# Turning two heads' marks and maxima at a time in an attention stage, with a new order of its look-ahead

## The chip, the cores and the metric

The kernel runs on one core of a Trainium2 chip. The metric is the device time of one execution in microseconds (us); lower is better. The engines are named as in the profile: PE is the tensor engine (PEld its weight loads), ACT the scalar engine, DVE the vector engine, POOL the GpSimd engine, SP the one that issues DMAs here.

## The reference

One decoder layer on x (1, 1024, 1024) in float32. After a modulated layer norm one projection gives all inputs of two attention sides and their gates:

```python
u = _layer_norm(x) * (1.0 + scale[:, None, :]) + shift[:, None, :]
(q_a, kv_cmp, kv_sel, kv_win, g_nsa, z_a,
 q_b, kv_b, z_b, g_merge) = _split_columns(u @ w_in[l])
...
o_cmp, p_cmp = _compressed_attention(qa, kc, vc)
sel_idx = _select_blocks(p_cmp, S)
o_sel = _selected_attention(qa, k_s, v_s, sel_idx)
o_win = _banded_attention(qa, k_w, v_w, NSA_WINDOW)
...
o_b = _banded_attention(qb, k_b, v_b, SWA_WINDOW, sinks[l]).reshape(B, S, SWA_WIDTH)
y_b = o_b * jax.nn.silu(z_b)
merged = jax.nn.sigmoid(gm_a) * (y_a @ w_up_a[l]) + jax.nn.sigmoid(gm_b) * (y_b @ w_up_b[l])
out = merged @ w_out[l]
x = _layer_norm(DEEPNORM_ALPHA * x + gate[:, None, :] * out) * ln_g[l] + ln_b[l]
```

Side a has 8 query heads in 2 groups of 4 (64 columns each) and three branches: compressed keys, the 8 best blocks of 64 keys, and a window of 512 keys. Side b has 8 heads in 2 groups, a window of 128 keys, and a sink for each head. All scores are scaled by 0.125 before their softmax.

## The kernel before

**Stages.** The layer norm and the first projections run until about 140 us. Then comes attention, until about 725 us, then the gating of its outputs, the two up projections, the output projection and the last norm.

**Units.** Attention works through 32 units in a fixed order: side a, group 0, query tiles 0 to 7 (128 rows each), then group 1, then the same for side b. A unit holds 4 heads. It has three parts.

- `C` turns the queries. ACT rounds them into `qat` and POOL puts what rounding leaves beside it; four transposes on PE (L759) give `qa`, copied by ACT (L761). In side a it then does the compressed branch: scores, a softmax over 64 columns, and for query tiles 4 and up the choice of blocks, whose marks (0 or -1e30 for 16 blocks) POOL writes into `qbt`.
- `M` finds each row's maximum: matmuls of `qa` with the keys, then DVE's passes over them (L878) and a reduction (L882) that writes the negated maxima of two branches into two columns of `qbt`. Then four transposes (L890), one for each head, and a copy by ACT (L892) give `qb`. Each of the two tiles `qbt` is 128 x (4 heads x 128): 64 columns of rounded queries (written by ACT, L755), 16 of marks, 2 of maxima, the rest zeros.
- For each tile of 128 keys, `score` makes two matmuls over all four heads, one of the keys' high parts with `qa` and one with `qb`, whose further rows add marks and maxima. Masked tiles get a pass of DVE (L907) and the exp by ACT (L909); others the exp alone (L911). ACT rounds the result to `ph` (L914) and POOL takes the rest `pl` (L917). `weigh` multiplies both with the values, and `combine` writes the unit's result.

**Order.** `run` emits these parts. While unit i is weighed, step by step, `part` emits a share of `M` for unit i + 1 and of `C` for unit i + 2, and both are finished with the unit. Each step also reports a planned time (0.43 for a score, 0.54 for a weighing, 0.22 for 512 columns of maxima, 0.25 for turning), and `feed` multiplies it with a ratio and emits that much of *fill*: matmuls that attention does not wait for (the next group's query projections, side b's keys and values, and blocks of 128 columns of the gates' projection). A fill block loads its weights with DMAs through three buffers, ACT rounds them (L259), POOL takes the rest (L260). `ratio` is 9.0 before the first unit, 0.9 in it, 1.25 in the rest of side a; in side b it spreads what is left over the remaining need. Four of the gates' blocks are kept for the stage after attention. A planner in the compiler then orders the instructions on each engine, with this order of emission as their priority.

Before the first unit, `values` brings the values of two branches to a common scale and splits them (four passes of ACT, four of DVE). The queries' rotation tables are scaled by 0.125 when they are made (L1173).

Of the kernel before, what the change touches and what calls it, by code (L numbers as in the profile page):

```python
# [20 lines left out]
NT = 8  # L21
# [6 lines left out]
POFF = math.log(16.0)  # L28
XB = 8
# [25 lines left out]
RATIO = {'start': 9.0, 'e': 0.9, 'a': 1.25, 'b': 1.0}  # L55
EU = 1
# [659 lines left out]
class Att:  # L716


    def __init__(self, L, q, work):

        self.L, self.q, self.w = L, q, work
        self.ms, self.st, self.av = Banks(L, MS), Banks(L, ST), Banks(L, (5,))
        nc = L.nc
        self.nc = nc
        self.U = {}
        self.qbt = []
        for i in range(2):
# [3 lines left out]
        self.p0 = work.tile([128, 128], F32, name="p0")[:, :68]  # L731
        nc.gpsimd.memset(self.p0, 0.0)
        self.n, self.last = 0, []
        self.off = [True, True]

    def rows_off(self, i):

        if not self.off[i]:
            self.nc.gpsimd.tensor_copy(self.qbt[i][:, :, 64:80],
                                       self.L.mk[:, 128:129, None].to_broadcast([128, 4, 16]))  # L740
            self.off[i] = True


    def C(self, u):
# [6 lines left out]
        qbt = st["qbt"] = self.qbt[self.n % 2]  # L751
# [3 lines left out]
        (nc.gpsimd.tensor_copy if QL == 2 else nc.scalar.copy)(qbt[:, :, 0:64], q)  # L755
# [4 lines left out]
        qa = st["qa"] = w.tile([128, 512], F32R, name="qa", tag="qa", bufs=3)  # L760
        nc.scalar.copy(qa, tr.bitcast(F32).rearrange("p h t -> p (h t)"))  # L761
        yield 0.25
        if side == "b":
            self.rows_off(self.n % 2)
            return
# [11 lines left out]
        nc.scalar.activation(e, t, AF.Exp)  # L777
# [4 lines left out]
        pc = w.tile([128, 4, 64], F32, name="cp", tag="cp")  # L782
# [25 lines left out]
        pT = w.tile([128, 2, 128], F32, name="pT", tag="pT")  # L808
# [20 lines left out]
    def M(self, u):  # L829
# [3 lines left out]
        qa, qbt = st["qa"], st["qbt"]  # L833
# [48 lines left out]
        nc.vector.tensor_reduce(qbt[:, :, 80:82], mx, axis=AX.X, op=OP.max, negate=True)  # L882
        if side == "b":
            es = st["es"] = w.tile([128, 2, 4], F32, name="esink", tag="esink", bufs=3)
            nc.gpsimd.tensor_tensor(es[:, 0], L.sink[:, g * 4:g * 4 + 4], qbt.bitcast(F32)[:, :, 80 + g], op=OP.add)
            nc.scalar.activation(es[:, 1], es[:, 0], AF.Exp, bias=L.poff)
        yield 0
        tr = self.ms.tile([128, 4, 128], F32R)
        for h in range(4):
            self.last.append(nc.tensor.transpose(tr[:, h, :], qbt[:, h, :], L.idr).ins)  # L890
        qb = st["qb"] = w.tile([128, 512], F32R, name="qb", tag="qb", bufs=2)
        nc.scalar.copy(qb, tr.bitcast(F32).rearrange("p h t -> p (h t)"))  # L892
        yield 0.25


    def score(self, u, br, kt):
# [9 lines left out]
        if kt == qt or edge:  # L906
            nc.vector.tensor_tensor(e.rearrange("p (h q) -> p h q", h=4), ps.rearrange("p (h q) -> p h q", h=4),  # L907
                                    L.mkt[:, int(edge), None, :].to_broadcast([128, 4, 128]), op=OP.add)
            nc.scalar.activation(e, e, AF.Exp, bias=L.poff)  # L909
        else:  # L910
            nc.scalar.activation(e, ps, AF.Exp, bias=L.poff)  # L911
# [48 lines left out]
    def run(self, units, fill, ratio, values):  # L960
# [52 lines left out]

        def part(f, u, k, n):
# [26 lines left out]
        for gi, grp in enumerate(groups):  # L1041
            u, bi = steps[grp[0]][:2]
            ui = units.index(u)
            side = "e" if ui < EU else u[0]
# [21 lines left out]
            if k == n:  # L1066
                if ui + 1 < len(units):
                    finish(self.M, units[ui + 1])
                if ui + 2 < len(units):
                    finish(self.C, units[ui + 2])  # L1070
# [53 lines left out]
def run_layer(L):  # L1124
# [22 lines left out]
    nc.sync.dma_start(L.sink, bass.AP(tensor=I["sinks"].tensor, offset=I["sinks"].offset, ap=[[0, 128], [1, 8]]))  # L1147
    acc = L.acc1
# [45 lines left out]
    def q_chunk(side, g, rows):  # L1194
# [3 lines left out]
        for t in ORD[side][g]:  # L1198
# [5 lines left out]
            L.rope(q, a[:, :256], t, qp, nc.vector, L.qcos, L.qsin)  # L1204
# [96 lines left out]
    for cm in (wk_cm, kvb[0], k0_cm, k1_cm, qp_cm):  # L1301
        L.close(cm)
# [214 lines left out]
```

## Time and profile before

| | us |
|---|---|
| median of 3 runs | 943.93 |
| lowest, highest | 943.79, 946.45 |
| the profiled execution | 945.29 |
| its span, first to last instruction | 943.5 |
| PE busy in the span | 914.3 |
| POOL, DVE, ACT busy | 575.6, 550.2, 471.4 |

The profiled execution is one run of its own; its time and its span differ by what lies before the first and after the last instruction. A busy time is the union of an engine's instructions. The ends of PE's matmuls are modelled, so a busy PE may still start its matmuls a little late. In the rows below, idle time stands ahead of the instruction that ended it, with the engine and line that released it.

### The profile page before, as it was taken

To read this page: it belongs to the slowest core of one execution; us is meant where nothing else is said; L and a number is where in the kernel's file an instruction comes from. 1 tells how busy PE (TensorE), PEld (TensorE's weight loads), DVE (VectorE), ACT (ScalarE), POOL (GpSimd) and SP (SyncE) were. 2 spreads that over 40 slices of the span, in tenths; PEclk is the share of its full clock that TensorE was granted. 3 is DMA by queue.
4 is the path that set the end of the run, shared out by engine and by line. 5 is a ranking of instruction groups with operands and counts; after the bars stand their busy time and mean duration, and the time that the engine had idled before them with its cause. 6 is when DMAs were issued, how large, how long until landed. Compare 5 with 4: busy or idle time off the path is not lost.

```text
span 943.5 us, 18610 instructions
## 1 busy us (share of the span) xinstructions
PE 914.3 (97%) x6592; PEld 787.0 (83%) x6592; DVE 550.2 (58%) x1621; ACT 471.4 (50%) x984; POOL 575.6 (61%) x808
## 2 busy tenths in 40 slices
PE   7899998999999999999999999999899999999996
PEld 5689997788899888898899888789788888888885
DVE  7843356554776554465786643456552666454687
ACT  5846344344555566646555555756663664532100
POOL 7867565365768766767677766756753245535822
PEclk9999999999999999999999999999989999999999
DMA  9913232212202211202201212030222977655312
GB/s 329 293 29 115 81 91 57 79 51 79 68 7 53 62 57 57 63 13 70 76 7 35 74 58 75 22 101 13 69 62 75 371 249 221 192 188 193 130 69 110
DMA packets 93278, 95.40 MB, mean 101 GB/s; under 512 B 7616, under 2 KB 72192, under 8 KB 93184
## 3 DMA queue, kind: packets, MB, share of 16 engines
q1 hardware_dynamic: 93184, 94.21, 31.9%
q8 instruction: 52, 0.85, 0.4%
q14 instruction: 42, 0.34, 0.1%
HBM read 73.21 MB, written 20.97 MB: 100 GB/s over the span
## 4 chain that ended last, share of the span: by engine, by line
PE 69%; DMA 8%; DVE 8%; POOL 7%; ACT 3%; issue 3%; SPq 1%; DVEq 0%; POOLq 0%; ACTq 0%
PE bank L108 65%; DMA sg<-gm_raw 2%; POOL z L1421 2%; DMA raw<-in_w_ada_dram 2%; DMA raw<-in_w_out_dram 1%; DMA raw<-in_w_in_dram 1%; POOL rstd L1444 1%; DVE res L1450 1%; POOL pl L917 1%; PE bank L890 1%; DVE jk L878 1%; DMA x<-in_x_dram 1%; PE bank L759 1%; POOL whl L260 1%; PE bank L1327 1%
## 5 line engine op out<-in xcount | busy, mean ns | idle before, releaser
L108 PE MATMUL bank<-whl,uH 128*128 128x256 f32 (+3 forms) x1168 | 270.6, 322 | 4.6 <-ACT uH L449 4.3
L108 PE MATMUL bank<-uH,whl 128*128 128x512 f32 x768 | 247.5, 397 | 0.0
L917 POOL TENSOR_TENSOR pl<-e,ph 128x512 f16<-128x512 f32 x162 | 188.1, 1167 | 66.4 <-ACT ph L914 58.1
L108 PEld LDWEIGHTS bank<-whl,uH 128*128 128x128 f32 x1168 | 197.9, 189 | 22.2 <-ACT uH L449 5.3
L108 PE MATMUL bank<-whl,uL 128*128 128x256 f32 (+3 forms) x584 | 181.3, 319 | 0.0
L108 PEld LDWEIGHTS bank<-uH,whl 128*128 128x128 f32 x768 | 142.1, 189 | 26.8
L260 POOL TENSOR_TENSOR whl<-raw,whl 128x256 fp32r<-128x256 f32 x128 | 99.1, 779 | 86.6 <-ACT whl L259 78.6
L108 PE MATMUL bank<-uL,whl 128*128 128x512 f32 x384 | 151.3, 394 | 0.0
L108 PEld LDWEIGHTS bank<-whl,uL 128*128 128x128 f32 x584 | 110.1, 189 | 7.4
L914 ACT CAST ph<-e 128x512 f16<-128x512 f32 x162 | 98.4, 618 | 25.1 <-PE bank L108 23.1
L878 DVE CUSTOM_DVE_ANT_0 jk<-bank,mk 128x256 bf16<-128x256 f32 (+3 forms) x168 | 73.9, 440 | 30.0 <-PE bank L108 25.4
L911 ACT ACTIVATE e<-bank,poff 128x512 f32<-128x512 f32 x92 | 62.0, 687 | 54.0 <-PE bank L108 50.3
L108 PEld LDWEIGHTS bank<-uL,whl 128*128 128x128 f32 x384 | 72.6, 189 | 14.9
L259 ACT CAST whl<-raw 128x256 fp32r<-128x256 f32 x128 | 50.8, 404 | 66.0 <-PE bank L108 42.2
L108 PE MATMUL bank<-yH,whl 128*128 128x512 f32 x256 | 79.1, 393 | 0.0
L108 PEld LDWEIGHTS <-pl 128*128 128x128 f16 x648 | 59.4, 98 | 17.1 <-issue 11.2
L249 POOL TENSOR_TENSOR whl<-raw,whl 128x256 fp32r<-128x256 f32 (+3 forms) x60 | 53.3, 895 | 24.1 <-ACT whl L248 22.8
L907 DVE TENSOR_TENSOR e<-bank,mkt 128x512 f32<-128x512 f32 x70 | 47.5, 688 | 33.0 <-PE bank L108 27.9
L108 PEld LDWEIGHTS <-ph 128*128 128x128 f16 x1296 | 65.2, 97 | 0.8 <-issue 0.5
L909 ACT ACTIVATE e<-e,poff 128x512 f32<-128x512 f32 x70 | 49.8, 721 | 30.5 <-DVE e L907 30.2
L248 ACT CAST whl<-raw 128x256 fp32r<-128x256 f32 (+3 forms) x72 | 34.2, 480 | 60.9 <-DMA raw<-in_w_out_dram 36.8
L108 PEld LDWEIGHTS bank<-yH,whl 128*128 128x128 f32 x256 | 47.7, 188 | 10.1 <-issue 0.5
(292 smaller groups left out, 1730.0 us busy)
## 6 DMA issues: line engine op xcount, KB each, us to landing
raw<-in_w_in_dram SPq DMA_DIRECT2D x136, 128.0 KB, 2.2
gm_raw<-gmo SPq DMA_DIRECT2D x48, 256.0 KB, 2.0
wada<-in_w_ada_dram SPq DMA_DIRECT2D x16, 512.0 KB, 6.0
sg<-gm_raw SPq DMA_DIRECT2D x32, 256.0 KB, 3.2
x<-in_x_dram SPq DMA_DIRECT2D x8, 512.0 KB, 5.1
o_raw<-q SPq DMA_DIRECT2D x32, 128.0 KB, 1.9
o<-o_raw SPq DMA_DIRECT2D x8, 512.0 KB, 6.7
z<-gm_raw SPq DMA_DIRECT2D x16, 256.0 KB, 6.7
```

The source lines that it names most:

```text
L108: return self.nc.tensor.matmul(out, l, r, start=start, stop=stop, skip_group_check=True)
L248: self.cast = nc.scalar.copy(h, raw).ins
L249: low = eng.tensor_tensor(l, raw, h.bitcast(F32), op=OP.subtract).ins
L259: nc.scalar.copy(hl[:, 0], raw)
L260: eng.tensor_tensor(hl[:, 1], raw, hl.bitcast(F32)[:, 0], op=OP.subtract)
L878: nc.vector.tensor_tensor_reduce(o, src, m, 1.0, -3e38, OP.add, OP.max, mx[:, h, g if side == "b" else bi, slots[h]:slots[h] + 1])
L907: nc.vector.tensor_tensor(e.rearrange("p (h q) -> p h q", h=4), ps.rearrange("p (h q) -> p h q", h=4), L.mkt[:, int(edge), None, :].to_bro ...
L909: nc.scalar.activation(e, e, AF.Exp, bias=L.poff)
L911: nc.scalar.activation(e, ps, AF.Exp, bias=L.poff)
L914: nc.scalar.copy(ph, e)
L917: eng.tensor_tensor(pl, e, ph, op=OP.subtract)
L1421: nc.gpsimd.tensor_scalar(z[:, t, :], z[:, t, :], ALPHA, None, op0=OP.mult)
```

## The change

Marks and maxima get a small tile of their own. `ex` is 128 x (4 heads x 32): 16 columns of marks, 2 of maxima, the rest zeros. Two heads are turned by one transpose, which gives 64 rows, and two copies by ACT put them into rows 64 to 95 of `qb`. The rounded queries no longer go through a second transpose: `C` copies them from its own transposes into rows 0 to 63 of `qb`, beside the copy that makes `qa`. `qb` is now one of three standing tiles (four in side b), whose rows 64 to 127 are cleared once, by DVE.

The scale of 0.125 moves from the rotation tables into the exps, and the sinks are divided by it once.

The scratch tiles of side a's compressed branch go to a pool of their own, which is closed when side b's first queries are turned; a fourth `qb`, a third `ex` and a fourth `qa` take its place.

The order: the first unit's `M` is emitted ahead of `values`. From side b's first unit on, while unit i is weighed, `M` of i + 1 is finished (its transposes and copies), `M` of i + 2 is emitted without them (`all_but`), and `C` of i + 3 is emitted. The fill's ratio is 1.5 in the first unit, 1.8 in side a's other units with query tile 0 to 3, and 1.05 in the rest of side a. The planned time for turning marks and maxima is 0.14.

```diff
-RATIO = {'start': 9.0, 'e': 0.9, 'a': 1.25, 'b': 1.0}
+RATIO = {'start': 9.0, 'e': 1.5, 's': 1.8, 'a': 1.05, 'b': 1.0}
...
-        self.qbt = []
-        for i in range(2):
-            q = work.tile([128, 4, 128], F32R, name=f"qbt{i}")
-            nc.gpsimd.tensor_copy(q.rearrange("p h d -> p (h d)"), L.mk[:, 128:129].to_broadcast([128, 512]))
-            self.qbt.append(q)
+
+        self.ex = [work.tile([128, 4, 32], F32R, name=f"ex{i}") for i in range(2)]
+        self.qb = [work.tile([128, 512], F32R, name=f"qb{i}") for i in range(3)]
+        for x in self.ex:
+            nc.gpsimd.tensor_copy(x.rearrange("p h c -> p (h c)"), L.mk[:, 128:129].to_broadcast([128, 128]))
+        for x in self.qb:
+            nc.vector.tensor_copy(x[64:128], L.mk[64:128, 128:129].to_broadcast([64, 512]))
...
-        qbt = st["qbt"] = self.qbt[self.n % 2]
+        if side == "a":
+            ex, qb = self.ex[self.n % 2], self.qb[self.n % 3]
+        else:
+            if len(self.ex) == 2:
+
+                L.close(self.wx_cm)
+                self.wx, self.wx_cm = L.pool("sideb", 1, side="right")
+                self.qb.append(self.wx.tile([128, 512], F32R, name="qb3"))
+                self.ex.append(self.wx.tile([128, 4, 32], F32R, name="ex2"))
...
-        (nc.gpsimd.tensor_copy if QL == 2 else nc.scalar.copy)(qbt[:, :, 0:64], q)
         yield 0
...
         nc.scalar.copy(qa, tr.bitcast(F32).rearrange("p h t -> p (h t)"))
+        nc.scalar.copy(qb[0:64], tr.bitcast(F32)[0:64].rearrange("p h t -> p (h t)"))
         yield 0.25
...
-        tr = self.ms.tile([128, 4, 128], F32R)
-        for h in range(4):
-            self.last.append(nc.tensor.transpose(tr[:, h, :], qbt[:, h, :], L.idr).ins)
-        qb = st["qb"] = w.tile([128, 512], F32R, name="qb", tag="qb", bufs=2)
-        nc.scalar.copy(qb, tr.bitcast(F32).rearrange("p h t -> p (h t)"))
-        yield 0.25
+        tr = self.ms.tile([128, 2, 128], F32R)
+        for j in range(2):
+            self.last.append(nc.tensor.transpose(tr[0:64, j, :], ex[:, 2 * j:2 * j + 2, :].rearrange("p h c -> p (h c)"),
+                                                 L.idr).ins)
+        rows = qb[64:96].rearrange("p (j i t) -> p i j t", j=2, i=2)
+        for i in range(2):
+            nc.scalar.copy(rows[:, i], tr.bitcast(F32)[i * 32:i * 32 + 32])
+        yield 0.14
...
-            nc.scalar.activation(e, ps, AF.Exp, bias=L.poff)
+            nc.scalar.activation(e, ps, AF.Exp, bias=L.poff, scale=SCALE)
...
+        def all_but(f, u):
+
+            s = get(f, u)
+            while s[1] < 3:
+                s[1] += 1
+                feed(next(s[0]))
...
+        def jobs(ui):
+
+            b = 2 * NT
+            if ui == b - 2:
+                return [(finish, self.C, b + 1, 0)]
+            if ui == b - 1:
+                return [(finish, self.M, b, -6), (finish, self.C, b + 2, -3), (all_but, self.M, b + 1, -1)]
+            if ui >= b:
+                e = EORD
+                return [(finish, self.M, ui + 1, e[0]), (all_but, self.M, ui + 2, e[1]), (finish, self.C, ui + 3, e[2])]
+            return []
+
         side = "start"
         finish(self.C, units[0])
+        finish(self.M, units[0])
         values()
         finish(self.C, units[1])
-        finish(self.M, units[0])
...
-            side = "e" if ui < EU else u[0]
+            side = "e" if ui < EU else "s" if u[0] == "a" and u[2] < 4 else u[0]
...
-            if ui + 1 < len(units):
+            if ui < 2 * NT - 1:
                 part(self.M, units[ui + 1], k, n)
-            if ui + 2 < len(units):
                 part(self.C, units[ui + 2], k, n)
+            for f, g, x, w in jobs(ui):
+                if x < len(units) and k == (w if w > 0 else n + w):
+                    f(g, units[x])
...
+    nc.gpsimd.tensor_scalar(L.sink, L.sink, 1.0 / SCALE, None, op0=OP.mult)
...
-    L.qcos = qp.tile([128, 8, 32], F32, name="qcos")
-    qsin = qp.tile([128, 2, 8, 32], F32, name="qsin")
-    L.qsin = (qsin[:, 0], qsin[:, 1])
-    for o, x in ((L.qcos, L.cos), (L.qsin[0], L.nsin), (L.qsin[1], L.sin)):
-        nc.scalar.mul(o, x, 0.125)
...
-            L.rope(q, a[:, :256], t, qp, nc.vector, L.qcos, L.qsin)
+            L.rope(q, a[:, :256], t, qp, nc.vector)
```

## Rows read from the trace of the kernel before

**Rows 1.** The page's first part: busy time of each engine in us, share of the span, instructions.

```profile
PE 914.3 (97%) x6592; PEld 787.0 (83%) x6592; DVE 550.2 (58%) x1621; ACT 471.4 (50%) x984; POOL 575.6 (61%) x808
```

**Rows 2.** Busy time of each engine (PE, PEld, DVE, ACT, POOL, with instructions) in stretches of attention and after it; then granted clock, DMA share, GB/s. The second number is the stretch's length.

```profile
140.00:200.00 60.00, 55.25 (x334) 46.92 (x333) 35.41 (x117) 25.48 (x56) 30.30 (x48) 1.00 0.23 60
200.00:600.00 400.00, 399.37 (x3472) 346.54 (x3471) 234.29 (x841) 224.54 (x443) 274.87 (x358) 1.00 0.18 53
600.00:675.00 75.00, 72.81 (x714) 64.99 (x713) 43.19 (x163) 49.42 (x106) 51.47 (x81) 1.00 0.16 47
675.00:700.00 25.00, 22.40 (x154) 18.22 (x153) 12.70 (x42) 15.27 (x33) 14.97 (x25) 0.86 0.26 70
700.00:725.00 25.00, 24.59 (x189) 20.41 (x189) 9.19 (x35) 11.02 (x23) 11.06 (x15) 1.00 0.19 53
725.00:900.00 175.00, 175.00 (x802) 144.71 (x801) 100.46 (x146) 70.82 (x133) 84.69 (x68) 1.00 0.65 214
```

**Rows 3.** The same view in three steps of 5 us inside side b; the number after POOL's is the granted clock.

```profile
680.00:685.00 5.00, 2.48 (x13) 1.96 (x14) 1.70 (x9) 4.63 (x11) 3.42 (x7) 0.83 0.34 81
685.00:690.00 5.00, 5.00 (x24) 4.04 (x24) 2.94 (x8) 3.47 (x7) 4.03 (x7) 0.50 0.00 0
690.00:695.00 5.00, 5.00 (x57) 4.07 (x55) 1.75 (x8) 1.60 (x4) 1.48 (x2) 0.98 0.32 105
```

**Rows 4.** Side b, 603 to 722 us: the stretch as a whole, then PE's groups there with count, busy us, mean ns, idle us before them and who ended that.

```profile
603.00:722.00 119.00, 114.12 (x993) 99.23 (x994) 64.02 (x235) 72.88 (x154) 74.69 (x117) 0.97 0.19 54
...
L108 PE MATMUL bank<-Vw,pl 128*128 128x65 f16 x72 | 8.8, 198 | 0.5 <-POOL pl L917 0.5
...
L108 PE MATMUL bank<-Vs,pl 128*128 128x65 f16 x60 | 7.0, 195 | 0.5 <-POOL pl L917 0.5
L890 PE MATMUL bank<-idr,qbt 128*128 128x128 f32 x56 | 6.8, 244 | 1.4 <-DVE qbt L882 1.4
L108 PE MATMUL bank<-Kw,qa 128*128 128x256 f32 (+1 forms) x32 | 6.6, 295 | 1.5 <-ACT qa L761 1.5
L759 PE MATMUL bank<-idr,qat 128*128 128x128 f32 x52 | 6.6, 246 | 1.2 <-DVE mx L878 1.2
```

**Rows 5.** Instructions in order of time at the start of attention (start us, us, engine, line, operation; in brackets the idle time before and who ended it).

```profile
140.98 1.16 POOL L729 CAST qbt<-mk 128x512 fp32r<-128x512 f32 x2
...
143.07 0.37 PE L759 MATMUL bank<-idr,qat 128*128 128x128 f32 x2 [0.79 <-POOL qat L753]
...
158.17 1.34 ACT L334 ACTIVATE Vs<-vrs,vmxs 128x512 f16<-128x512 f32 x2
...
161.55 0.71 PE L108 MATMUL bank<-vcb,pT 128*128 128x128 f32 x4 [1.52 <-ACT pT L809]
...
189.94 0.54 PE L890 MATMUL bank<-idr,qbt 128*128 128x128 f32 x4 [0.63 <-DVE qbt L882]
```

**Rows 6.** The same view of PE, around transposes of L890: a pair and four, each with the matmul that starts next.

```profile
601.12 0.29 PE L890 MATMUL bank<-idr,qbt 128*128 128x128 f32 x2
601.24 0.34 PE L759 MATMUL bank<-idr,qat 128*128 128x128 f32 x2
...
672.36 0.46 PE L890 MATMUL bank<-idr,qbt 128*128 128x128 f32 x4
672.66 0.21 PE L108 MATMUL bank<-Vw,pl 128*128 128x65 f16 x1
```

**Rows 7.** Groups of the whole span by line, tiles and shape: count, busy us, mean ns, idle before.

```profile
L892 ACT CAST qb<-bank 128x512 fp32r<-128x512 f32 x32 | 18.8, 586 | 22.4 <-PE bank L890 22.2
...
L890 PE MATMUL bank<-idr,qbt 128*128 128x128 f32 x128 | 15.8, 245 | 2.0 <-DVE qbt L882 2.0
...
L755 ACT CAST qbt<-q 128x256 fp32r<-128x256 f32 x32 | 13.1, 409 | 0.1
...
L809 ACT COPY pT<-bank 128x256 f32<-128x256 f32 x16 | 5.9, 369 | 14.1 <-PE bank L807 14.1
...
L309 ACT CAST Kw<-bank 64x256 fp32r<-64x256 f32 x12 | 4.4, 364 | 5.5 <-DVE Kw L308 5.3
```

**Rows 8.** ACT in order of time in side b, and the PE row that follows.

```profile
680.37 0.40 ACT L259 CAST whl<-raw 128x256 fp32r<-128x256 f32 x1 [1.48 <-DMA raw<-in_w_in_dram]
680.68 0.72 ACT L909 ACTIVATE e<-e,poff 128x512 f32<-128x512 f32 x1
681.30 0.56 ACT L761 CAST qa<-bank 128x512 fp32r<-128x512 f32 x1
...
681.92 0.50 PE L108 MATMUL bank<-Kw,qa 128*128 128x256 f32 x2 [1.55 <-ACT qa L761]
```

**Rows 9.** The first scaling of the rotation tables (duration ns min/median/max, start us), and POOL's sum of sinks and maxima in side b.

```profile
L1173 ACT ACTIVATE qcos<-cos x1: 413/413/413, 63.4 to 63.4; 128x256 f32<-128x256 f32 x1
...
L885 POOL TENSOR_TENSOR esink<-sink,qbt 128x4 f32<-128x4 f32 x14 | 2.9, 204 | 2.7 <-DVE qbt L882 2.7
```

**Rows 10.** ACT's groups in side b, 603 to 722 us, with the idle time before them.

```profile
L909 ACT ACTIVATE e<-e,poff 128x512 f32<-128x512 f32 x31 | 21.7, 720 | 16.3 <-DVE e L907 16.2
...
L892 ACT CAST qb<-bank 128x512 fp32r<-128x512 f32 x15 | 8.8, 585 | 8.4 <-PE bank L890 8.2
L761 ACT CAST qa<-bank 128x512 fp32r<-128x512 f32 x14 | 8.1, 578 | 5.3 <-PE bank L759 5.3
L259 ACT CAST whl<-raw 128x256 fp32r<-128x256 f32 x17 | 6.8, 405 | 11.2 <-PE bank L108 6.0 <-DMA raw<-in_w_in_dram 5.0
```

More of the change, by code (lines that the diff above doesn't have):

```diff
@@ L28 @@
 POFF = math.log(16.0)
+SCALE = 0.125
+EORD = (1,0,1)
 XB = 8
@@ L725, in __init__ @@
         self.U = {}
-        self.qbt = []
-        for i in range(2):
-            q = work.tile([128, 4, 128], F32R, name=f"qbt{i}")
-            nc.gpsimd.tensor_copy(q.rearrange("p h d -> p (h d)"), L.mk[:, 128:129].to_broadcast([128, 512]))
-            self.qbt.append(q)
+        self.ex = [work.tile([128, 4, 32], F32R, name=f"ex{i}") for i in range(2)]
[4 more added lines that the diff above has]
+            nc.vector.tensor_copy(x[64:128], L.mk[64:128, 128:129].to_broadcast([64, 512]))
         self.p0 = work.tile([128, 128], F32, name="p0")[:, :68]
+        self.wx, self.wx_cm = L.pool("sidea", 1, side="right")
         nc.gpsimd.memset(self.p0, 0.0)
@@ L738, in rows_off @@
         if not self.off[i]:
-            self.nc.gpsimd.tensor_copy(self.qbt[i][:, :, 64:80],
+            self.nc.gpsimd.tensor_copy(self.ex[i][:, :, 0:16],
                                        self.L.mk[:, 128:129, None].to_broadcast([128, 4, 16]))
@@ L750, in C @@
         self.n += 1
-        qbt = st["qbt"] = self.qbt[self.n % 2]
+        if side == "a":
[6 more added lines that the diff above has]
+                self.ex.append(self.wx.tile([128, 4, 32], F32R, name="ex2"))
+                nc.gpsimd.tensor_copy(self.ex[2].rearrange("p h c -> p (h c)"), L.mk[:, 128:129].to_broadcast([128, 128]))
+                nc.vector.tensor_copy(self.qb[3][64:128], L.mk[64:128, 128:129].to_broadcast([64, 512]))
+                self.nb = 0
+            i = (1, 2, 0)[self.nb % 3]
+            if i < 2:
+                self.rows_off(i)
+            ex, qb = self.ex[i], self.qb[(2, 3, 0, 1)[self.nb % 4]]
+            st["n"] = self.nb
+            self.nb += 1
+        st["ex"], st["qb"] = ex, qb
         nc.scalar.copy(qat[:, :, 0, :], q)
@@ L759, in C @@
             self.last.append(nc.tensor.transpose(tr[:, h, :], qat[:, h].rearrange("p a d -> p (a d)"), L.idr).ins)
-        qa = st["qa"] = w.tile([128, 512], F32R, name="qa", tag="qa", bufs=3)
+        if side == "b" and st["n"] % 4 == 1:
+            qa = self.wx.tile([128, 512], F32R, name="qa3", tag="qa3")
+        else:
+            qa = w.tile([128, 512], F32R, name="qa", tag="qa", bufs=3)
+        st["qa"] = qa
         nc.scalar.copy(qa, tr.bitcast(F32).rearrange("p h t -> p (h t)"))
+        nc.scalar.copy(qb[0:64], tr.bitcast(F32)[0:64].rearrange("p h t -> p (h t)"))
         yield 0.25
         if side == "b":
-            self.rows_off(self.n % 2)
             return
@@ L776, in C @@
         e = t
-        nc.scalar.activation(e, t, AF.Exp)
+        nc.scalar.activation(e, t, AF.Exp, scale=SCALE)
         yield 0.45
@@ L832, in M @@
         st = self.U[u]
-        qa, qbt = st["qa"], st["qbt"]
+        qa, ex, qb = st["qa"], st["ex"], st["qb"]
         brs = self.branches(u)
@@ L1066, in run @@
             if k == n:
-                if ui + 1 < len(units):
+                if ui < 2 * NT - 1:
                     finish(self.M, units[ui + 1])
-                if ui + 2 < len(units):
                     finish(self.C, units[ui + 2])
@@ L1300, in run_layer @@
     fill.rest()
-    for cm in (wk_cm, kvb[0], k0_cm, k1_cm, qp_cm):
+    for cm in (A.wx_cm, wk_cm, kvb[0], k0_cm, k1_cm, qp_cm):
         L.close(cm)
```

26 lines of the change are left out of this document (13 added, 13 removed).

## The prediction

> **What bounds the kernel now.** I read the page's busy shares first: PE is busy 97% of 943.5 us and the next engine, POOL, 61% [rows 1]. That is an average over stages, so the table by stretch comes next [rows 2]. From 200 to 600 us, the long units of side a, PE is idle 400.00 - 399.37 = 0.63 us; from 725 to 900 us not at all. What a change is worth there is the PE time that it takes out. Two stretches differ. From 140 to 200 us, where attention starts, PE is idle 60.00 - 55.25 = 4.75 us. From 600 to 725 us, which is side b, it is idle (75.00 - 72.81) + (25.00 - 22.40) + (25.00 - 24.59) = 5.20 us. Inside the latter the granted clock drops: 0.83, 0.50 and 0.98 in three steps of 5 us [rows 3], which loses 5 x (0.17 + 0.50 + 0.02) = 3.45 us of full clock; the drop follows a stretch in which PE was busy 2.48 of 5 us.
>
> Who ended those idle times shows in PE's rows. In side b: the reduction of the maxima (DVE L882) before the transposes of L890, 1.4 us; the copy of the turned queries (ACT L761), 1.5 us; the mask pass of DVE (L878), 1.2 us; the low halves (POOL L917), 1.0 us in two rows [rows 4]. At the start: 0.79 us for POOL's qat, 1.52 us for ACT's pT, 0.63 us for DVE's maxima [rows 5]. So PE's work bounds most of attention, and short chains through ACT, DVE and POOL bound its two ends.
>
> **The change part by part.** The sum is made against the profiled execution, 945.29 us with a span of 943.5 us; it stands 1.36 us above the median of the three runs, 943.93, so I take the saving off the median. A difference of 0.3%, 2.8 us, is about what a measurement of this kernel can tell from no change.
>
> *Two transposes less for each of 32 units.* Each unit has four transposes of `qbt` (x128 in all), and keeps two of half the width. Their cost by starts: a pair that starts at 601.12 us is followed by the next matmul at 601.24, 0.12 us; four in a row take 672.66 - 672.36 = 0.30 us [rows 6]. A pair is thus 0.12 us, and 32 x 0.12 = 3.84 us of PE leave. From below, nothing, if PE would wait in their place; from above, half of the group's 15.8 us of busy time, 7.9 us [rows 7]. I take 3.8, since the starts say what PE's queue really gives up, and PE has 0.63 us of idle time in 400.
>
> *ScalarE's copies.* Out go a copy of 128x256 (409 ns, L755) and one of 128x512 (586 ns, L892). In come a copy of 64x512 and two of 32x256. Columns set the price, not partitions: 64x256 took 364 ns and 128x256 369 ns [rows 7]. So 586 + 2 x 369 - 409 - 586 = +329 ns for a unit, 32 x 0.329 = +10.5 us of ACT. [...] What hides it: ACT is busy 224.54 of 400 us in the long units [rows 2] and 72.88 of 119 us in side b [rows 4], where 16 x 0.329 = 5.3 us are added. I take 0 on the path; without that cover it is 5.3 us in side b (the rival below). The chain maxima to `qb` keeps its length: two pieces are 2 x 369 - 586 = 0.15 us longer, two transposes 0.12 us shorter.
>
> *Start of attention.* POOL's two fills of `qbt`, 1.16 us, stand before the subtraction that PE waited 0.79 us for [rows 5]; they become two of a quarter of the size on POOL and three of 64x512 on DVE, so that wait should nearly go. The first unit's maxima are asked for ahead of the values' split; before, the split's two ACT passes (1.34 us) and weight casts stood in ACT's queue ahead of pT, for which PE waited 1.52 us. More fill in the short units (1.5 for the first and 1.8 for the others with qt < 4, after 0.9 and 1.25) gives PE other matmuls there. What is late next: DVE, which gets the three fills, and ACT's weight casts, which wait for transfers. Of the 4.75 us of idle time I take 1.5 off; bounds: all 4.75 off, or 2 us added if 1.34 us of split and 0.7 us of fills land before the first weighing.
>
> *Side b's look-ahead.* Queries are turned three units ahead and maxima reduced two ahead, their transposes one ahead; today it is two and one. This takes aim at the waits on L882, L761 and L878: 1.4 + 1.5 + 1.2 = 4.1 us. It does not touch why ACT was late at 681 us: its cast of a weight waited 1.48 us for a transfer, and the exp and the copy of `qa` behind it started only at 680.68 and 681.30, PE at 681.92 [rows 8]. With `qa` a unit earlier PE does not need that copy at that moment, but the weighing still needs the exp. If the hole shrinks, the clock stays up. Of 5.20 + 3.45 = 8.65 us I take 3.2; bounds: all 8.65 off, or 5.3 added (ACT's copies in series).
>
> *Fill moved.* By the planner's own costs the short units after the first are 59.8 and the long ones 116.7 units of time. Fill in side a was 0.9 x 4.9 + 1.25 x 176.5 = 225 and becomes 1.5 x 4.8 + 1.8 x 59.1 + 1.05 x 115.5 = 235: 10 us of matmuls leave side b. The total of matmuls stays; only the cover moves. Long units get 1.05 after 1.25 and had 0.63 us of idle time: 0, at most 4 added if the idle share of side b's first 75 us (2.2 in 75) spread over a third of them.
>
> *The rest.* Three ACT scalings at 63 us go, the first of 413 ns; the scale rides in the exp's own multiplier, and a POOL operation on eight sinks is added (the nearest row, the sink's sum on 128x4, took 204 ns) [rows 9]. PE worked on the first projection then; 0, bounds 3 x 0.41 = 1.2 off and 0.2 added. The pool that is closed and opened at side b makes two fills wait for side a's last probabilities; they are a unit old by then: 0.
>
> Sum: 3.8 + 1.5 + 3.2 = 8.5 us off, 943.9 - 8.5 = 935.4.
>
> **The rivals.** *ScalarE's queue becomes side b's bound (slower).* ACT's work stood behind a late cast once already [rows 8]. It was busy 72.88 of 119 us there, and the rest was waiting: 16.3 us before the exp of masked tiles, 8.4 before `qb`, 5.3 before `qa`, 11.2 before the casts [rows 4, 10]. If these waits stay, the 5.3 us of copies come in series, and with 10 us less fill to cover them PE idles and the clock drops once more (3.45). Price: + 5.3 + 3.45 - 1.9 (side a's 16 units of transposes) - 1.5 = +5.4, 949.3 us. It decides once ACT's work and its waits, 73 + 5.3 + 41 = 119 us, exceed what PE has in side b: 114.12 us less 10 of fill and 1.9 of transposes, 102. That is near, and it speaks for it; against it, the waits for `qb` and `qa` are just what a longer look-ahead takes away, and blocks of fill kept for later can be drawn forward. [...]
>
> *The stalls only move (no change).* Transposes are saved, but idle time comes back behind the weight transfers, or in long units with less fill: -3.8 + 2 to 4, 942 to 944. For it: the longest hole in side b began at a transfer, and a new order on every engine makes new holes.
>
> *All of it goes.* Every idle microsecond of both ends and the lost clock: 3.8 + 4.75 + 8.65 = 17.2, 926.7 us. Against it: waits on L917 and on transfers aren't addressed.
>
> **How the numbers follow.** Forecast, 4 to 13 us off (931 to 940): 0.64. All goes (below 931): 0.13. Stalls move: 0.13. Slower through ACT: 0.10. The range of 8 in 10 runs from 928 to 944: it leaves out the lower part of the second case, about 0.06, and the last. Faster by over 0.3%: 0.64 + 0.13 = 0.77; within: 0.13; slower: 0.10.
>
> **What would show it.** The transposes' group at half its count, with near half its busy time; ACT's busy time up by about 10 us; PE idle from 140 to 200 us near 3 us; side b's PE rows without L882 and with a granted clock of 1.00 throughout. It is wrong if PE's rows in side b show longer waits for ACT's e, `qa` or the new copies, if the long units get idle time above 3 us, or if the clock drops in a new place.

## The result, and the profile after

The kernel after takes 933.31 us (median of four runs, 932.80 to 935.59), the kernel before 944.77 in the same comparison (943.79 to 946.45). The ratio is 0.9882 [0.9864, 0.9900]: 1.2% or 11.1 us faster. The forecast was 935.4 us. The profiled execution of after is its slowest run, 935.59 us with a span of 933.9, so the two traces differ by 9.6 us, and it is these 9.6 us that the rows below divide up.

The busy line of the page of after, beside [rows 1]:

```profile
PE 906.9 (97%) x6528; PEld 777.6 (83%) x6528; DVE 558.6 (60%) x1625; ACT 484.4 (52%) x1013; POOL 573.9 (61%) x810
```

PE was busy 914.3 us before. It lost 7.4 us of busy time and (943.5 - 914.3) - (933.9 - 906.9) = 2.2 us of idle time, together 9.6. ACT is 13.0 us busier. Lines of code have moved: L110 is the matmul helper and L261 a fill weight's rounding (L108 and L259 before), L781 and L787 the queries' transposes and copy (L759 and L761 before), L904 and L908 DVE's passes and reduction (L878 and L882), L916 and L920 the transposes and copies of marks and maxima (L890 and L892), L935 the mask pass, L937 and L939 the exps, L945 the low halves.

The kernel after by stretches, beside [rows 2, 3]: length; busy time of PE, PEld, DVE, ACT and POOL; granted clock, DMA share, GB/s.

```profile
140.00:200.00 60.00, 57.73 (x352) 49.64 (x351) 35.95 (x118) 23.31 (x53) 29.16 (x46) 1.00 0.26 71
200.00:600.00 400.00, 398.93 (x3417) 344.61 (x3416) 240.87 (x854) 232.12 (x465) 275.03 (x362) 1.00 0.19 54
600.00:725.00 125.00, 120.75 (x1079) 102.44 (x1078) 67.85 (x237) 85.68 (x181) 80.52 (x122) 0.99 0.20 58
690.00:695.00 5.00, 5.00 (x41) 4.05 (x40) 2.44 (x8) 2.49 (x6) 3.72 (x6) 0.66 0.25 62
```

PE's idle time goes from 4.75 to 2.27 us at the start of attention, from 0.63 to 1.07 in the long units, and from 5.20 to 4.25 in side b. The granted clock still drops once in side b, now at 690 us and for half as long: 5 x 0.34 = 1.7 us of full clock are lost, where 3.45 were. A 128x512 matmul of after is followed by the next in 0.42 us within the drop (691.81 to 692.23) and in 0.23 us behind it (693.74 to 693.97). Take the lost clock off PE's busy time and its work is, as an estimate, 914.3 - 3.45 = 910.9 us before and 906.9 - 1.7 = 905.2 after, 5.7 less. The account: 5.7 of work, 1.7 of clock, 2.2 of idle time. The same reckoning, with the clock lost from 140 us on taken off, gives 903.9 to 907.9 us in the ten variants below that have the same 6528 matmuls; so the 5.7 us of work are good to about 2 us.

The changed operations over the whole span, beside [rows 7]: count, busy us, mean ns, idle time before.

```profile
L920 ACT CAST qb<-bank 32x256 fp32r<-32x256 f32 x64 | 23.1, 361 | 25.7 <-PE bank L916 24.8
...
L787 ACT CAST qa<-bank 128x512 fp32r<-128x512 f32 x32 | 18.7, 584 | 17.0 <-PE bank L781 16.6
L788 ACT CAST qb<-bank 64x512 fp32r<-64x512 f32 x32 | 18.5, 579 | 0.0
...
L916 PE MATMUL bank<-idr,ex 128*64 128x128 f32 x64 | 9.3, 227 | 0.0
```

PE's groups in side b (603 to 719 us) that waited over 0.2 us, beside [rows 4]:

```profile
L110 PE MATMUL bank<-qb,Kw 128*128 128x512 f32 x20 | 8.7, 444 | 2.1 <-ACT qb L920 2.1
...
L110 PE MATMUL bank<-qa,Kw 128*128 128x512 f32 x20 | 8.0, 414 | 0.4 <-DVE e L935 0.4
...
L110 PE MATMUL bank<-Kw,qa 128*128 128x256 f32 (+1 forms) x32 | 6.2, 285 | 1.0 <-DVE mx L904 1.0
```

The waits for the reduced maxima (1.4 us at the transposes) and for `qa` (1.5) are gone; DVE's passes (L904) are still waited for, 1.0 us. The largest wait is a new one: PE now waits for ACT's copies of the turned rows. One place of it, ACT and then PE in order of time:

```profile
688.00 0.72 ACT L937 ACTIVATE e<-e,poff 128x512 f32<-128x512 f32 x1
688.74 0.73 ACT L920 CAST qb<-bank 32x256 fp32r<-32x256 f32 x2
...
689.53 0.50 PE L110 MATMUL bank<-qb,Kw 128*128 128x512 f32 x1 [1.19 <-ACT qb L920]
```

The copies stand behind an exp in ACT's queue, and PE starts as the second one ends; the clock falls some 0.5 us later.

### The profile page after: what moved, and what is told of

The parts are those of the page before. It is cut to its first block, busy times and chain, and to the rows that moved or that the text cites. A ratio compares the mean times of both kernels' runs of the same rounds, so it can differ in the third digit from the quotient of the medians.

```text
span 933.9 us, 18524 instructions
## 1 busy us (share of the span) xinstructions
PE 906.9 (97%) x6528; PEld 777.6 (83%) x6528; DVE 558.6 (60%) x1625; ACT 484.4 (52%) x1013; POOL 573.9 (61%) x810
## 4 chain that ended last, share of the span: by engine, by line
PE 85%; DVE 5%; ACT 3%; POOL 3%; DMA 2%; issue 1%; DVEq 0%; POOLq 0%; ACTq 0%
PE bank L110 82%; DMA x<-in_x_dram 1%; POOL rstd L1489 1%; DMA raw<-in_w_in_dram 1%; DVE res L1495 1%; PE bank L781 1%; PE bank L1372 1%; DVE stats L1481 1%; DVE z L1480 1%; DVE gt L1479 1%; DVE lnst L534 1%; ACT lnT L448 0%; ACT qb L920 0%; PE bank L833 0%; ACT lnT L474 0%
## 5 line engine op out<-in xcount | busy, mean ns | idle before, releaser
L110 PE MATMUL bank<-whl,uH 128*128 128x256 f32 (+3 forms) x1168 | 269.2, 322 | 5.0 <-ACT uH L451 4.6
L110 PE MATMUL bank<-uH,whl 128*128 128x512 f32 x768 | 247.9, 397 | 0.1
L945 POOL TENSOR_TENSOR pl<-e,ph 128x512 f16<-128x512 f32 x162 | 188.9, 1173 | 75.4 <-ACT ph L942 66.5
L110 PEld LDWEIGHTS bank<-whl,uH 128*128 128x128 f32 x1168 | 197.5, 189 | 22.6 <-ACT uH L451 5.7
L110 PE MATMUL bank<-whl,uL 128*128 128x256 f32 (+3 forms) x584 | 181.4, 319 | 0.0
L110 PEld LDWEIGHTS bank<-uH,whl 128*128 128x128 f32 x768 | 141.8, 189 | 26.5 <-issue 0.2
L110 PE MATMUL bank<-uL,whl 128*128 128x512 f32 x384 | 151.6, 395 | 0.0
L110 PEld LDWEIGHTS bank<-whl,uL 128*128 128x128 f32 x584 | 110.2, 189 | 7.1
L904 DVE CUSTOM_DVE_ANT_0 jk<-bank,mk 128x256 bf16<-128x256 f32 (+3 forms) x168 | 73.7, 438 | 27.8 <-PE bank L110 23.4
L110 PEld LDWEIGHTS bank<-uL,whl 128*128 128x128 f32 x384 | 72.5, 189 | 14.3
L261 ACT CAST whl<-raw 128x256 fp32r<-128x256 f32 x128 | 50.8, 403 | 64.6 <-PE bank L110 47.2
L939 ACT ACTIVATE e<-bank,poff 128x512 f32<-128x512 f32 x92 | 61.9, 687 | 40.6 <-PE bank L110 32.9
L110 PE MATMUL bank<-yH,whl 128*128 128x512 f32 x256 | 79.3, 392 | 0.0
L110 PEld LDWEIGHTS <-pl 128*128 128x128 f16 x648 | 59.3, 98 | 18.4 <-issue 12.5
L935 DVE TENSOR_TENSOR e<-bank,mkt 128x512 f32<-128x512 f32 x70 | 48.0, 689 | 39.7 <-PE bank L110 20.6
L110 PEld LDWEIGHTS <-ph 128*128 128x128 f16 x1296 | 65.3, 97 | 0.7
L937 ACT ACTIVATE e<-e,poff 128x512 f32<-128x512 f32 x70 | 50.5, 723 | 20.5 <-DVE e L935 20.1
L1311 DVE COPY gmo<-bank 128x512 f32<-128x512 f32 x48 | 33.0, 688 | 42.0 <-PE bank L110 39.9
```

The costliest lines, as they stand in the source:

```text
L110: return self.nc.tensor.matmul(out, l, r, start=start, stop=stop, skip_group_check=True)
L261: nc.scalar.copy(hl[:, 0], raw)
L904: nc.vector.tensor_tensor_reduce(o, src, m, 1.0, -3e38, OP.add, OP.max, mx[:, h, g if side == "b" else bi, slots[h]:slots[h] + 1])
L937: nc.scalar.activation(e, e, AF.Exp, bias=L.poff, scale=SCALE)
L939: nc.scalar.activation(e, ps, AF.Exp, bias=L.poff, scale=SCALE)
L945: eng.tensor_tensor(pl, e, ph, op=OP.subtract)
```

## The experiments

My theory was that the copies on ACT cost nothing because other work covers them, and that the gain comes from transposes, start and look-ahead, each with its own term. The main rival was that ACT's queue bounds side b. Each edit is made to the kernel after, and each ratio stands against the kernel before, with its 95% interval. The moved scale and the new pools stay in every variant, so what they are worth by themselves is not shown. Where two ratios are subtracted, I give as uncertainty the root of the sum of the squared half widths, and turn it into time with 946 us.

**Turning alone.** The old order, ratios, planned time and first maxima; what is left of the change is `ex`, the two transposes and the copies, with the standing tiles, the pools and the moved scale.

```diff
-RATIO = {'start': 9.0, 'e': 1.5, 's': 1.8, 'a': 1.05, 'b': 1.0}
+RATIO = {'start': 9.0, 'e': 0.9, 's': 1.25, 'a': 1.25, 'b': 1.0}
...
-        yield 0.14
+        yield 0.25
...
-        finish(self.M, units[0])
         values()
         finish(self.C, units[1])
+        finish(self.M, units[0])
...
-            if ui < 2 * NT - 1:
+            if ui + 1 < len(units):
                 part(self.M, units[ui + 1], k, n)
+            if ui + 2 < len(units):
                 part(self.C, units[ui + 2], k, n)
-            for f, g, x, w in jobs(ui):
-                if x < len(units) and k == (w if w > 0 else n + w):
-                    f(g, units[x])
...
```

> The new turning alone: the kernel after with the old ratios, the old place of the first maxima, the old look-ahead in side b and the old planned time of 0.25. Theory 1 (each part pays what the prediction priced): only the transposes are saved, 3.8 us, ratio 0.996 to the kernel before, with the transposes' group at half its count. Theory 2 (the gain is all order and cover, the transposes were hidden): ratio 0.999 to 1.001. Theory 3 (ScalarE's added copies cost time in side b): 1.002 or more.

Measured: 1.0018 [1.0003, 1.0032], 947.72 us, between the ranges of the second theory and the third. Its stretch of side b, and the PE groups there that waited for ACT's copies:

```profile
600.00:725.00 125.00, 114.02 (x1000) 97.52 (x1000) 64.71 (x238) 82.15 (x177) 77.19 (x119) 0.99 0.18 52
```

```profile
L110 PE MATMUL bank<-qb,Kw 128*128 128x512 f32 x19 | 6.9, 415 | 0.9 <-ACT qb L920 0.9
...
L110 PE MATMUL bank<-Kw,qa 128*128 128x256 f32 (+1 forms) x32 | 6.5, 289 | 1.9 <-DVE mx L904 0.8 <-ACT qa L787 0.7 <-DVE cf L977 0.4
...
L110 PE MATMUL bank<-qb,Ks 128*128 128x512 f32 x15 | 5.8, 405 | 0.6 <-ACT qb L920 0.6
L110 PE MATMUL bank<-Ks,qa 128*128 128x256 f32 x24 | 4.8, 297 | 2.3 <-ACT qa L787 2.0 <-ACT qb L920 0.3
```

PE is idle 10.98 us there, 5.8 more than before. PE waits 2.7 us for `qa`, 1.5 in the kernel before, and some 1.8 for the new copies of the rows. The prediction had priced ACT's copies in series at 5.3 us. So turning by itself is no gain: side b gives back what the transposes save. (This profiled execution, 949.83 us, is the highest of its 12 runs, so the 5.8 us are at the upper end.)

**Look-ahead undone**, all else kept: queries two units ahead, maxima one.

```diff
-            if ui < 2 * NT - 1:
+            if ui + 1 < len(units):
                 part(self.M, units[ui + 1], k, n)
+            if ui + 2 < len(units):
                 part(self.C, units[ui + 2], k, n)
-            for f, g, x, w in jobs(ui):
-                if x < len(units) and k == (w if w > 0 else n + w):
-                    f(g, units[x])
...
-                if ui < 2 * NT - 1:
+                if ui + 1 < len(units):
                     finish(self.M, units[ui + 1])
+                if ui + 2 < len(units):
                     finish(self.C, units[ui + 2])
...
```

> The kernel after with side b's look-ahead undone: maxima one unit ahead, queries two. Theory 1: it loses 3.2 us of the 11 gained, ratio 0.9915, with PE's waits for the reduction of the maxima back in side b. Theory 2 (order and cover carry the gain, most of it in side b): it loses 6 us or more, ratio 0.9945. A rival to both (the look-ahead is worth nothing, since the fill's cover does the work): 0.988.

Measured: 1.0025 [1.0011, 1.0038]. The whole gain is gone, and 1.43 ± 0.22% or 13.5 us lie between this kernel and the kernel after. Its side b, and the PE groups that waited most between 600 and 725 us:

```profile
600.00:725.00 125.00, 113.05 (x1032) 96.08 (x1029) 66.41 (x238) 84.82 (x178) 78.10 (x118) 0.97 0.16 46
```

```profile
L110 PE MATMUL bank<-uH,whl 128*128 128x512 f32 x103 | 33.9, 406 | 1.9 <-ACT whl L261 1.9
L110 PE MATMUL bank<-Vw,pl 128*128 128x65 f16 x80 | 9.8, 200 | 2.0 <-POOL pl L945 2.0
...
L110 PE MATMUL bank<-qa,Kw 128*128 128x512 f32 x20 | 8.7, 445 | 2.6 <-DVE e L935 1.2 <-ACT e L939 1.1
L110 PE MATMUL bank<-qb,Kw 128*128 128x512 f32 x20 | 7.5, 434 | 1.7 <-ACT qb L920 1.7
```

PE is idle 11.95 us, and half of that is for what ACT makes (5.8 us: weights, exps, `qb`, `qa`); 3.1 us are for DVE and 2.8 for POOL's `pl`. No single operand is late, many are. The traced execution took 945.27 us, the lowest of 12: 7.7 us more idle time here and 1.7 us more lost clock than in the trace of after nearly make up the 9.6 us between the two spans. The other eleven had a mean granted clock of 0.983 to 0.988 where this one had 0.990, so the rest of the 13.5 us may be clock; no trace shows it.

**Turning and look-ahead together**, with the old ratios, the old place of the first maxima and the old planned time:

```diff
-RATIO = {'start': 9.0, 'e': 1.5, 's': 1.8, 'a': 1.05, 'b': 1.0}
+RATIO = {'start': 9.0, 'e': 0.9, 's': 1.25, 'a': 1.25, 'b': 1.0}
...
-        yield 0.14
+        yield 0.25
...
-        finish(self.M, units[0])
         values()
         finish(self.C, units[1])
+        finish(self.M, units[0])
```

> The turning and side b's look-ahead together, without the new ratios and with the first maxima behind the values' split (planned time 0.25). Undoing one part each cost 13.5 us (look-ahead), 6.8 (ratios) and 4.3 (first maxima), 24.6 in all, for 11.1 gained, while the turning alone lost 1.7. Theory 4 (the look-ahead is what makes up for ScalarE's copies, and the other two then add their own): about 0.9882 + 0.0072 + 0.0046 = 1.000 if their worth adds; Theory 5 (look-ahead pays its own 1.4% also without the others, and they overlap): 1.0018 - 0.0143 = 0.9875 to 0.992.

Measured: 0.9900 [0.9886, 0.9915]. Against turning alone the look-ahead is worth 1.18 ± 0.21%, 11.2 us. Its trace has 5.3 us of idle time between 600 and 725 us and a clock of 1.00 there. These two parts make 1.0% of the 1.2%.

**Whose queue it is.** Turning alone once more, with side b's row copies on DVE; then the kernel after with the same edit.

```diff
-            nc.scalar.copy(rows[:, i], tr.bitcast(F32)[i * 32:i * 32 + 32])
+            (nc.vector.tensor_copy if side == "b" else nc.scalar.copy)(rows[:, i], tr.bitcast(F32)[i * 32:i * 32 + 32])
```

> The new turning alone (as in the first run of this study), with side b's two copies of the turned rows on DVE. Theory 3b (in side b ScalarE's added copies, 5.3 us in series, ate the saving of the transposes): side b's idle time of PE falls back from 11.0 to about 6 us, ratio 0.996 to 0.998. A rival (the longer path from the maxima to qb, two pieces in series on whatever engine): 1.001 to 1.003.

> The kernel after with side b's two copies of the turned rows on DVE. PE's longest waits left in side b are for these copies on ScalarE (2.1 us). If ScalarE's queue is what is left of side b's limit: PE idle from 600 to 725 us falls from 4.25 to about 2 us and the clock stays up (1.7 us), ratio 0.984 to 0.986. If DVE then takes ScalarE's place: 0.988 or more.

Measured without the look-ahead: 0.9936 [0.9921, 0.9950], 0.82 ± 0.21% or 7.8 us faster than with ACT. That is more than was expected, and the rival (a longer path on whatever engine, 1.001 to 1.003) is out. Side b of that kernel, and its largest wait:

```profile
600.00:725.00 125.00, 118.86 (x1039) 101.69 (x1039) 78.55 (x271) 71.82 (x148) 77.84 (x120) 1.00 0.20 55
```

```profile
L110 PE MATMUL bank<-qb,Kw 128*128 128x512 f32 x18 | 6.7, 426 | 4.7 <-DVE qb L920 4.7
```

ACT has 10.3 us less to do in this stretch, PE's idle time falls from 10.98 to 6.14, and the clock drop at 657 us (1.7 us) is not there. Most of what is left is waiting for the same copies, now DVE's. With the look-ahead: 0.9871 [0.9853, 0.9890], not to be told from the 0.9882 of after. Its side b and its largest wait:

```profile
600.00:725.00 125.00, 120.71 (x1081) 102.39 (x1081) 78.62 (x269) 74.26 (x149) 79.98 (x121) 0.99 0.20 61
```

```profile
L110 PE MATMUL bank<-qb,Kw 128*128 128x512 f32 x20 | 8.8, 448 | 2.5 <-DVE qb L920 2.5
```

ACT loses 11.4 us of work again, and PE's idle time stays (4.25 and 4.29); neither of the two expectations, about 2 us of idle time or a ratio of 0.988 and more, was met. The four kernels answer the question as far as the copies go: on ACT they cost 7.8 us more than on DVE when maxima and queries are one and two units ahead, and no more than on DVE (0.11 ± 0.26%) when they are two and three ahead. The rival's mechanism is real, and the look-ahead is what pays for it. What remains with the look-ahead is a wait for the copies on whichever engine makes them, 2.1 us on ACT and 2.5 on DVE; whether DVE's own queue has taken ACT's place there is not shown.

One copy of each pair on DVE, the other on ACT, with the look-ahead:

```diff
-            nc.scalar.copy(rows[:, i], tr.bitcast(F32)[i * 32:i * 32 + 32])
+            (nc.vector.tensor_copy if side == "b" and i else nc.scalar.copy)(rows[:, i], tr.bitcast(F32)[i * 32:i * 32 + 32])
```

> The kernel after with side b's two copies of the turned rows on two engines, one on ScalarE and one on DVE, side by side. The two in series took 0.73 us, and PE's longest waits in side b are for them: if their length is what is late, 0.983 to 0.986; if it is the place in either engine's queue, 0.987 to 0.989 as with both on DVE.

Measured: 0.9924 [0.9911, 0.9937], slower than either whole version and than both expectations. PE idles 7.2 us between 600 and 725 us, 2.8 of them for the copies that DVE ends, and the clock drops at 688. The loads don't explain it: ACT's 79.2 us and DVE's 72.6 lie between those of the two whole versions. Every variant gets an order of its own, so I read it as the size of what a new order does by itself, some 0.4%; that is argued, not shown. A pair that has to wait in two queues is a rival that no run here separates from it.

**Which half of the look-ahead.** Queries three ahead with maxima one ahead; then queries two ahead with maxima two ahead.

```diff
-                return [(finish, self.M, b, -6), (finish, self.C, b + 2, -3), (all_but, self.M, b + 1, -1)]
+                return [(finish, self.M, b, -6), (finish, self.C, b + 2, -3)]
...
-                return [(finish, self.M, ui + 1, e[0]), (all_but, self.M, ui + 2, e[1]), (finish, self.C, ui + 3, e[2])]
+                return [(finish, self.M, ui + 1, e[0]), (finish, self.C, ui + 3, e[2])]
```

> The kernel after with half of the look-ahead: queries are still turned three units ahead, but the maxima of a unit are asked for only one ahead, with its transposes. If PE's waits for DVE's passes and the reduction are what the look-ahead takes away, most of the 13.5 us come back: ratio 0.996 to 1.002. If ScalarE's copies of the queries are: 0.989 to 0.991.

```diff
-            if ui == b - 2:
-                return [(finish, self.C, b + 1, 0)]
...
-                return [(finish, self.M, b, -6), (finish, self.C, b + 2, -3), (all_but, self.M, b + 1, -1)]
+                return [(finish, self.M, b, -6), (finish, self.C, b + 1, -3), (all_but, self.M, b + 1, -1)]
...
-                return [(finish, self.M, ui + 1, e[0]), (all_but, self.M, ui + 2, e[1]), (finish, self.C, ui + 3, e[2])]
+                return [(finish, self.M, ui + 1, e[0]), (finish, self.C, ui + 2, e[2]), (all_but, self.M, ui + 2, e[1])]
```

> The other half: maxima two units ahead, queries two ahead, turned just before them. If the waits for the reduction carry the gain: 0.989 to 0.992. If the copies of the queries do: 0.996 to 1.002, with PE waiting for qa.

Measured: 0.9945 [0.9928, 0.9963] and 0.9962 [0.9948, 0.9977]. Beside the kernel with neither (1.0025) the queries are worth 0.80% and the maxima 0.63%. The sum, 1.43%, is what both give together. So neither half is there for the other's sake, as far as some 0.3% of uncertainty lets one see. The first ratio lies in neither of its two ranges, and the waits are not the ones expected: with queries alone PE waits most for POOL's `pl` (3.6 us from 600 to 725 us), with maxima alone for ACT's row copies (2.9) and the reduction (1.5), and not for `qa`. That again speaks for queues that run late rather than for one operand.

**The transposes by themselves.** The two narrow transposes are issued twice, into the same place:

```diff
-        for j in range(2):
+        for j in (0, 1, 0, 1):
```

> The kernel after with each unit's two transposes issued twice into the same places: the old count of transposes at the new shape, nothing else added. Theory 1a: 32 x 0.12 = 3.8 us more, ratio 0.992. If transposes are hidden beside waits in part: 2 us, ratio 0.990.

Measured: 0.9908 [0.9893, 0.9923], 0.26 ± 0.23% or 2.5 us slower than after. Its clock does not drop in side b, so wall time flatters it by the 1.7 us that after loses: the two traces are 936.1 - 933.9 = 2.2 us apart, 3.9 with that. PE's busy line on its page:

```profile
PE 909.9 (97%) x6592; PEld 781.9 (84%) x6592; DVE 560.1 (60%) x1625; ACT 484.0 (52%) x1013; POOL 574.9 (61%) x810
```

909.9 us of work against the 905.2 of after are 4.7 us for 64 transposes, good to about 2 us by the spread above. The starts are the better measure. A run of four, then the next matmul, in this kernel:

```profile
404.16 0.41 PE L916 MATMUL bank<-idr,ex 128*64 128x128 f32 x4
404.41 0.69 PE L110 MATMUL bank<-uH,whl 128*128 128x512 f32 x2
```

and a run of two in the kernel after:

```profile
308.50 0.28 PE L916 MATMUL bank<-idr,ex 128*64 128x128 f32 x2
308.62 0.45 PE L110 MATMUL bank<-whl,uH 128*128 128x256 f32 x2
```

These are 0.25 us and 0.12 us. Over all such runs in the two traces the medians are 0.243 and 0.122 us: 32 x 0.121 = 3.9 us, what wall time and lost clock give too.

**Turning undone, the new order kept**: `qbt`, four transposes and one copy again, ACT's rounding into `qbt` and POOL's fills of it too, with a third `qbt` in side b.

```diff
+        nc.scalar.copy(qbt[:, :, 0:64], q)
...
-        for j in range(2):
-            self.last.append(nc.tensor.transpose(tr[0:64, j, :], ex[:, 2 * j:2 * j + 2, :].rearrange("p h c -> p (h c)"),
-                                                 L.idr).ins)
...
-            nc.scalar.copy(rows[:, i], tr.bitcast(F32)[i * 32:i * 32 + 32])
+        for h in range(4):
+            self.last.append(nc.tensor.transpose(tr[:, h, :], qbt[:, h, :], L.idr).ins)
...
+        nc.scalar.copy(qb, tr.bitcast(F32).rearrange("p h t -> p (h t)"))
...
```

> The kernel after with the turning undone: four transposes and one copy of 128x512 for a unit, the rounded queries through qbt again (a third qbt in side b), with the new order, ratios and look-ahead kept. The first runs put the new turning alone at 1.0018 and the kernel without the look-ahead at 1.0025. Theory 1a (the transposes pay 3.8 us once side b waits less, the added copies are hidden): ratio 0.992 to 0.993. Theory 3a (the added copies of ScalarE cost as much as the transposes give, also with the look-ahead): 0.987 to 0.989, so the order alone carries the gain.

Measured: 0.9948 [0.9932, 0.9964]. In the new order the turning is worth 0.66 ± 0.24%, 6.2 us, where in the old order it cost 1.7. That is about what the transposes save (5.8 us, below), so little of the copies' cost is left in this order. Its side b has 4.51 us of idle time, about that of after. A stall in the up-projection that after does not have is part of the 6.2 us (PE's group between 725 and 770 us):

```profile
L110 PE MATMUL bank<-yH,whl 128*128 128x512 f32 x43 | 13.0, 397 | 1.7 <-DVE gmo L1306 1.7
```

**The old ratios**, and **the first maxima behind the values' split**, each alone:

```diff
-RATIO = {'start': 9.0, 'e': 1.5, 's': 1.8, 'a': 1.05, 'b': 1.0}
+RATIO = {'start': 9.0, 'e': 0.9, 's': 1.25, 'a': 1.25, 'b': 1.0}
```

> The kernel after with the fill's ratios of before (0.9 in the first unit, 1.25 in the rest of side a). Theory 1: the spread of the fill is worth about 1 us of the 1.5 at the start, ratio 0.989, and PE's idle time from 140 to 200 us grows by 1 us. Theory 2: it carries a good part of the gain, 4 us or more lost, ratio 0.992 or above.

```diff
-        finish(self.M, units[0])
         values()
         finish(self.C, units[1])
+        finish(self.M, units[0])
```

> The kernel after with the first unit's maxima asked for behind the values' split and the second unit's queries, as before. Theory 1: 0.5 us lost, ratio 0.9885 to 0.989, no difference that can be told. Theory 2: the start's idle time of 4.75 us comes back, 2 us or more lost, ratio 0.9905.

Measured: 0.9954 [0.9936, 0.9973] and 0.9928 [0.9908, 0.9949], that is 0.72 ± 0.26% and 0.46 ± 0.27% slower than after. The start of attention with the old place of the first maxima:

```profile
140.00:200.00 60.00, 55.32 (x326) 46.77 (x325) 36.88 (x120) 25.53 (x56) 30.49 (x48) 0.97 0.22 60
```

PE idles 4.68 us, 2.4 more than after, and the clock loses 60 x 0.03 = 1.8: 4.2 us. This trace does not lose the 1.7 us of clock that after loses in side b, which leaves the 2.5 us between the two traces (936.4 and 933.9); by the medians it is the 0.46%, 4.4 us. With the old ratios the long units idle 3.83 us instead of 1.07, and the start loses clock as well; side b is better, with 2.65 us of idle time and no drop. In all PE idles 2.2 us more there (29.2 and 27.0), half of the 4.6 us between the traces (938.5 and 933.9); what the rest is stays open. The second price is about as large as what a new order may do by itself. But with both undone (the kernel with turning and look-ahead) the loss is only 0.18 ± 0.23%. The two prices are prices in this order, and can't be added.

## Why the prediction was right, and where its steps were not

**The total** was 2.1 us too high, from terms that the account above puts otherwise: 5.7 of work, 2.48 at the start, 0.95 and 1.7 in side b, less 0.44 in the long units and 0.83 ahead of 140 us, 9.6 in all where the forecast had 3.8 + 1.5 + 3.2 = 8.5.

**Transposes: right in kind, a third too small.** 3.8 was taken. A unit's four took 0.30 us by starts [rows 6], its two take 0.12 now, so 32 x 0.18 = 5.8 us left, beside 5.7 us of work in the account and 6.2 us by the kernel with the turning undone (its stall included). The step that failed is "a pair is thus 0.12 us": that is what two cost, and the doubled pair confirms it (3.9 us), but what leaves is four wide ones less two narrow ones, and the rows had both, 0.30 - 0.12 = 0.18. The group's count halved as forecast; its busy time went from 15.8 to 9.3, not quite to half.

**ScalarE's copies: the price was right, "0 on the path" was not.** Columns set the price, as said: 361 ns for 32x256, 579 and 584 for 64 and 128 partitions of 512 columns. The copies that came less those that went are 23.1 + 18.5 - 13.1 - 18.8 = +9.7 us, after a forecast of 10.5. ACT's busy time rose by 13.0, but a busy time counts instructions that overlap once: the durations of all its instructions rose by 8.7 us (522.8 to 531.5), so the rest is neighbours that overlap less. The cover was argued from ACT's free share, 72.88 of 119 us, and turning alone shows that this share does not hide the copies: side b's idle time rose by 5.8 us, about the 5.3 that the step kept for the case without cover, and with the copies on DVE 7.8 us came back. The rival's condition was met by its own numbers (73 + 5.3 + 41 = 119 us of work and waits against 102) and was called near; as a test it says little, for in the kernel before ACT's work and waits came to 73 + 41 = 114 of 119 us already. The rival got 0.10, for a mechanism that does decide without the look-ahead.

**Look-ahead: right net, far too small alone.** 3.2 us were taken. In the traces side b gives 5.20 - 4.25 = 0.95 of idle time and 1.7 of clock, 2.7 net. Measured as a part it is worth 11 to 13.5 us, since it also pays for the copies. The prediction wrote 0 and 3.2 where some 6 to 8 lost and 11 gained belonged, and the errors cancelled. That the total came out so near is in this part luck. The wait moved where its sign for a wrong prediction pointed (the new copies, 2.1 us), and the clock drop came in a new place; neither undid the gain, as L882's 1.4 us and L761's 1.5 are gone. The third wait that it aimed at, 1.2 us for DVE's passes (L878, which the prediction calls the mask pass), is nearly all there still: 1.0 us at L904.

**Start of attention.** 1.5 taken, 2.5 of idle time measured; the steps hold in the main: the wait for POOL's `qat` went from 0.79 to 0.4 us and that for `pT` from 1.52 to 0.5, and undoing the first maxima alone brings 2.4 us back. What is late next there is DVE's `cp` (1.3 us of PE's 2.27), which the prediction named only as DVE's load. Ahead of 140 us, PE idles 0.8 us more than before, which the prediction took as nothing.

**Fill moved.** 0 taken; the long units idle 0.44 us more. From 140 to 600 us fill keeps PE busy 7.8 us longer (314.2 after 306.4), where 10 were forecast. The old ratios alone cost 0.7%, once the rest is in place; no step had that.

## What to carry to other kernels

An engine's free share does not say that more work on it is hidden: ACT's was 46 of 119 us in side b here, and with the turning alone PE idled 5.8 us more there. Price the work in series, in the stage where the engine's waits are long, and ask which other part of the change takes those waits away: here one part cost 6 to 8 us and another gave 11, and neither number was visible in the sum. To know what a part is worth, run it alone and undo it from the whole; where the two disagree (turning: +1.7 us alone, -6.2 in the new order), it is the order around it that is being measured.

## What was not expected of the hardware

It was not expected how often the clock drops, and how much that is beside the differences measured. The kernel after around its drop: length, busy times, granted clock.

```profile
687.00:690.00 3.00, 1.77 (x9) 1.11 (x10) 1.67 (x9) 2.94 (x8) 3.00 (x7) 1.00 0.45 121
690.00:694.00 4.00, 4.00 (x24) 3.09 (x23) 2.28 (x7) 1.95 (x4) 3.72 (x6) 0.57 0.27 65
```

PE was busy 1.77 of the 3 us ahead of it; then 4 x 0.43 = 1.7 us of full clock are lost. In the kernel before the same view reads 1.17 of 3 us busy, and 7 x 0.48 = 3.4 us lost. Drops of one or the other size came at 144, 182, 190, 611, 657 and 686 to 700 us in the variants. One of 1.7 us is two thirds of the 2.5 us that separate the doubled transposes from the kernel after, so the granted clock of both kernels has to be read before a ratio this small means anything. It has to be read by stretch: nine of the variants' traces show a granted clock of 0.98 between 0 and 140 us and three show 1.00, and yet PE is busy there for 128.1 to 130.6 us in the nine and for 128.7 to 130.8 in the three.
